# TensorE's order in the state-space scan written out by hand, with dense thirds between its parts

## The chip, the cores and the metric

The kernel runs on one core of one Trainium2 chip. The metric is the device time of one execution in microseconds. The core has a matrix engine (TensorE, PE in the profile, with its weight loads as PEld), a vector engine (VectorE, DVE), a scalar engine (ScalarE, ACT), GpSimd (POOL) and SyncE (SP), which issues most DMAs from one queue. Every engine works its own queue in order; an instruction that waits holds back what stands behind it.

## The reference, cut to what matters

One step of a hybrid decoder layer: a prompt of 1024 tokens and 8 single-token samples. One input projection feeds a state-space branch and a gated-delta branch; gates merge them, and a dense feed-forward and a per-layer input follow. The change lies in the state-space branch:

```python
proj = einsum('bld,de->ble', rms_norm(x), w_in)
z, xbc, dt_raw, qkv, gate, b_raw, a_raw, mgate = split(proj)
xbc = silu(causal_conv(xbc, ...)); xs, bm, cm = split(xbc)
# in chunks of the tokens, h = head, 8 heads in each of 4 groups g
lmat = exp(where(tril, acum_l - acum_s, -inf))            # decay in the chunk
cb = einsum('lgd,sgd->gls', cm, bm)
y_diag = einsum('gls,ghls,sghp->lghp', cb, lmat, xs*dt)   # diagonal product
chunk_states = einsum('lgd,lgh,lghp->ghpd', bm, exp(acum_last - acum), xs*dt)
state = state * exp(acum_last) + chunk_states             # from chunk to chunk
y_off = einsum('lgd,ghpd,lgh->lghp', cm, state_before, exp(acum))
y = (y_diag + y_off + xs * D) * silu(z)
y = rms_norm over each group (y)
```

The reference writes this with chunks of 64; the kernel uses 128.

## The kernel before, in words

**Layout.** Activations lie with channels on the 128 partitions and tokens along the row. Every dense product is done in three passes, with weights and activations each split in a high and a low part. `load_w` brings a weight tile (128 output channels by 1024 inputs, 512 KB) on SyncE's queue into `wraw` (2 buffers); ScalarE casts the high half `wh` (L138) and VectorE subtracts it for `wl` (L139), four of eight blocks at a time, three buffers each. `dense` runs over three thirds of the 1032 tokens (`CHUNKS`, 344 each); a third is 8 blocks times 3 matmuls, 24 in a row into one of three PSUM buffers `pd`, and is then evacuated by `evac`. Other PSUM pools: `pt` (2 buffers: transposes and small products), `py` (2), `pz` (1). All matmuls go through a helper at L69.

**Stages of the state-space branch.** Four groups g of eight heads. For each: `ssm_conv_group` projects and convolves B, C and four tiles X (18 dense thirds; taps on VectorE L411, silu on ScalarE L412, evacuation L397); `ssd` scans eight chunks; `fill` computes the raw output gates that later stages read (four weight tiles in group 0, three in groups 1 to 3, by the table `FILL`), evacuated into `mg` (L270); eight `ssm_dec` decode steps; `ssm_gate` projects four z tiles, multiplies X by silu(z) and sums squares. The root of these is applied beside the next group's convolutions.

**One chunk of `ssd`.** The row of decays is broadcast from DRAM to all partitions (`ab`, 512 KB, DMA L661, pool `sw` with 2 buffers), masked on GpSimd (L662), put through eight exponentials on ScalarE (L666) and multiplied on VectorE by the product CB (L680). The four X tiles are transposed into one `pt` (L669), scaled by VectorE into `xdt` (L672) and `xdd` (L674); CB and the transposed B share another `pt`, B is copied to `btok` (L679). Then the products: the diagonal one into `py` from `ab` and `xdt`; the off-diagonal one into another `py` from the state `st` and C; the chunk's state into `pz` from `btok` and `xdd`. VectorE carries the state on, multiplies the off-diagonal part by `eb` (a second broadcast, L691) and adds the diagonal one into X; GpSimd adds the rest (L711).

**What sets the order.** Nothing is placed by hand in before: the framework's scheduler lays the instructions of the whole program into the engines' queues. The code of `ssd` has no dense work, and `fill` stands behind it; the scheduler puts thirds of the fills between the scan's instructions and ahead of them.

**What precedes.** Ahead of group 0's scan stand the last in-chunk solve of the gated-delta branch (`solve(1)`: 31 steps on VectorE, L542 and L545; its matrix is copied on GpSimd, L547, and put out to DRAM, L548) and the transposes of the gated-delta convolution states (`states`, L419, six of them with four small transposes each, copied on ScalarE at L421 into `cso`, which has one buffer, and put out). Group 3 has the same transposes for the state-space branch. `ssm_dec_start` transposes the decode rows `bdec` and `cdec` (L592).

Of the kernel before, what the change touches and what calls it, by code (L numbers as in the profile page):

```python
# [8 lines left out]
F32 = mybir.dt.float32  # L9
# [7 lines left out]
P = 128  # L17
# [22 lines left out]
def hybrid_step(  # L40
# [108 lines left out]
    def dense(wt, acts, evac, chunks=CHUNKS):  # L149
        n = len(acts)  # L150
        for t0, tn in chunks:
# [8 lines left out]
            evac(t0, tn, o)  # L160

# [106 lines left out]
    def raw_proj(col, dst):  # L268
        t = mgp.tile([P, NT], F32, name="mg")
        dense(load_w(w_in[:, col : col + P], 8), hacts, lambda t0, tn, o: S.copy(t[:, t0 : t0 + tn], o))  # L270
        dma(dst, t)

    def fill(lo, hi):
        """gates of both branches and of the mix, put out as they are"""
        for j in range(lo, hi):
            if j < 16:
                raw_proj(COL_M + j * P, sg_d[j])
            else:
                raw_proj(COL_G + (j - 16) * P, gate_d[j - 16])
# [147 lines left out]
    def gate_proj(col, out, dec, func):  # L427
        def ev(t0, tn, o):
            n = min(tn, NP - t0)
            S.activation(out[:, t0 : t0 + n], o[:, :n], func)  # L430
            if n < tn:
                S.activation(dec, o[:, n:], func)

        dense(load_w(w_in[:, col : col + P], 8), hacts, ev)

# [130 lines left out]
    def norm_small(t, n, group, scale):  # L566
        """reciprocal root of the means of squares over the partitions and `group` tiles."""
# [31 lines left out]
    def ssm_dec(i):  # L599
        """step i: four rows of the batch, one pair of heads"""  # L600
# [34 lines left out]
    with (  # L635
# [19 lines left out]
        def ssd(g, Bt, Ct, X):  # L655
            st = None
            h0 = 8 * g
            for c in range(NC):
                cs = slice(c * C, c * C + C)
                ab = sw.tile([P, 8, C], F32, name="ab")  # L660
                dma(ab, acum_d[h0 : h0 + 8, cs].partition_broadcast(P))  # L661
# [3 lines left out]
                for h in range(8):  # L665
                    S.activation(ab[:, h], ab[:, h], AF.Exp, bias=ncolA[:, c, h0 + h : h0 + h + 1])  # L666
                t = pt.tile([P, 512], F32, name="pt")
# [13 lines left out]
                yd = py.tile([P, 512], F32, name="py")  # L681
                for h in range(8):
# [587 lines left out]
```

## Time and profile before

| | us |
|---|---|
| median of 3 runs | 2751.8 |
| lowest, highest | 2751.22, 2755.93 |
| span of the profiled execution | 2748.0 |
| TensorE busy in it | 2641.6 |
| VectorE, ScalarE, GpSimd busy | 1553.3, 996.6, 247.3 |

The profiled execution's own time is its span, 2748.0 us, and the little that lies around it; the median of the runs is 3.8 us above that span. A row of a timeline gives start, duration, engine, line, operation, the tiles written and read with their shapes, a count, and in brackets the idle time of the engine ahead of it with what ended it. A row of the table by stretches gives the stretch, its width, the busy time (and instructions) of PE, PEld, DVE, ACT and POOL, the clock that TensorE was granted (1.00 is full speed), the mean busy share of the DMA engines, and GB/s. A row of the chain gives start, duration and what the end of the program hung on at that time. Line numbers L are those of the kernel before, unless the changed kernel is named.

### The profile page before, as it was taken

The page shows a single profiled execution, that of the slowest core. Times are in us where ns is not written, and L with a number is a line of the kernel's source. Part 1 is how long each engine was busy: PE and PEld are TensorE (multiplying, and loading weights), DVE is VectorE, ACT ScalarE, POOL GpSimd, SP SyncE. Part 2 cuts the span into 40 slices and gives each one's busy share as a digit, 9 for nine tenths or more (in the row PEclk, how much of TensorE's full clock was granted, in tenths as well). Part 3 has the DMA queues.
Part 4 walks back from the last instruction along what each step waited for, and adds up shares of the span by engine and source line. Part 5 has one row for each costly group of instructions (what it writes and reads, how often), then busy time and mean ns, then how long its engine had stood idle before and what let it go on. Part 6 is the DMA issues. An engine that isn't in the chain of part 4 may idle for free.

```text
span 2748.0 us, 43742 instructions
## 1 busy us (share of the span) xinstructions
PE 2641.6 (96%) x17431; PEld 2551.2 (93%) x17431; DVE 1553.3 (57%) x2754; ACT 996.6 (36%) x2045; POOL 247.3 (9%) x493
## 2 busy tenths in 40 slices
PE   7999999879889889999999999999999999999998
PEld 7999999879779779899999999999999999999998
DVE  6677896767655655663554566434343333333465
ACT  5455544356343343342343225423212121212243
POOL 0101121030210210111010000011000000000020
PEclk9999999999999999999999999999999999999999
DMA  3355443445462462356685438411111111111122
GB/s 122 122 155 175 139 148 111 114 110 154 91 155 85 90 156 85 98 145 195 195 238 166 117 118 272 154 53 47 47 47 43 51 43 51 43 50 43 50 88 92
DMA packets 456665, 306.34 MB, mean 111 GB/s; under 512 B 44049, under 2 KB 430010, under 8 KB 455438
## 3 DMA queue, kind: packets, MB, share of 16 engines
q1 hardware_dynamic: 454062, 295.13, 37.5%
q10 hardware_dynamic: 2400, 8.42, 0.8%
q8 instruction: 137, 2.24, 0.3%
q14 instruction: 66, 0.54, 0.1%
HBM read 227.17 MB, written 76.31 MB: 110 GB/s over the span
## 4 chain that ended last, share of the span: by engine, by line
PE 80%; DMA 8%; DVE 5%; issue 3%; ACT 3%; POOL 1%; SPq 0%; DVEq 0%; POOLq 0%; ACTq 0%
PE pd L69 71%; DMA ab<-acum_d 5%; PE py L69 4%; PE pt L69 2%; PE pz L69 1%; ACT ab L666 1%; POOL ab L662 1%; DVE sd L614 1%; DMA wraw<-in_w_pl_gate_dram 1%; DVE wl L139 1%; DVE sdj L619 1%; DMA sd<-in_state_ssm_dram 0%; ACT wh L138 0%; DMA out_dram<-sd 0%; DMA bc<-bcd_d 0%
## 5 line engine op out<-in xcount | busy, mean ns | idle before, releaser
L69 PE MATMUL pd<-h,wh 128*128 128x344 f32 x6384 | 1552.2, 324 | 7.0 <-ACT wh L138 5.2
L69 PEld LDWEIGHTS pd<-h,wh 128*128 128x128 f32 x6384 | 1112.3, 189 | 24.1 <-issue 11.8
L69 PE MATMUL pd<-h,wl 128*128 128x344 f32 x3192 | 1038.1, 325 | 11.4 <-DVE wl L139 11.0
L69 PEld LDWEIGHTS pd<-h,wl 128*128 128x128 f32 x3192 | 604.3, 189 | 19.7 <-DVE wl L139 14.0
L138 ACT CAST wh<-wraw 128x512 fp32r<-128x512 f32 (+1 forms) x386 | 235.7, 612 | 844.3 <-PE pd L69 821.6
L139 DVE TENSOR_TENSOR wl<-wraw,wh 128x512 fp32r<-128x512 f32 (+1 forms) x386 | 264.8, 687 | 349.4 <-ACT wh L138 339.5
L69 PE MATMUL pd<-gu,wh 128*128 128x344 f32 (+2 forms) x1056 | 249.3, 320 | 0.1
L69 PE MATMUL pd<-y,wh 128*128 128x344 f32 x768 | 186.8, 324 | 0.0
L69 PEld LDWEIGHTS pd<-gu,wh 128*128 128x128 f32 x1056 | 182.4, 188 | 0.5 <-DVE acc L1108 0.4
L69 PE MATMUL pd<-gu,wl 128*128 128x344 f32 (+2 forms) x528 | 168.9, 320 | 0.0
L666 ACT ACTIVATE ab<-ab,ncolA 128x128 f32<-128x128 f32 x256 | 81.0, 392 | 150.7 <-POOL ab L662 150.7
L69 PEld LDWEIGHTS pd<-y,wh 128*128 128x128 f32 x768 | 132.6, 188 | 1.1 <-issue 0.2
L397 ACT COPY raw<-pd 128x344 f32<-128x344 f32 x144 | 63.2, 441 | 180.0 <-PE pd L69 176.2
L69 PE MATMUL pd<-y,wl 128*128 128x344 f32 x384 | 124.9, 325 | 0.0
L1159 DVE TENSOR_TENSOR acc<-acc,pd 128x344 f32<-128x344 f32 x120 | 61.3, 512 | 104.0 <-PE pd L69 103.5
L1138 DVE TENSOR_TENSOR lt<-rb,pd 128x344 f32<-128x344 f32 x66 | 33.9, 513 | 141.4 <-PE pd L69 141.4
L1094 POOL TENSOR_TENSOR sqs<-sqs,sqt 128x1032 f32<-128x1032 f32 x12 | 30.4, 2537 | 923.8 <-ACT sqt L1093 923.8
L69 PEld LDWEIGHTS pd<-gu,wl 128*128 128x128 f32 x528 | 99.2, 188 | 0.0
L411 DVE SCALAR_TENSOR_TENSOR ca<-raw,cwg,ca 128x1056 f32<-128x1056 f32 x72 | 96.3, 1338 | 0.9
L411 DVE SCALAR_TENSOR_TENSOR ca<-raw,cwm,ca 128x1056 f32<-128x1056 f32 x72 | 95.1, 1321 | 1.7
L69 PE MATMUL pd<-h,gw 128*128 128x384 f32 (+1 forms) x576 | 94.3, 322 | 1.7 <-DVE pg L1189 1.7
L69 PEld LDWEIGHTS pd<-h,gw 128*128 128x128 f32 x576 | 91.2, 188 | 2.7 <-DVE pg L1189 2.1
(387 smaller groups left out, 3444.5 us busy)
## 6 DMA issues: line engine op xcount, KB each, us to landing
wraw<-in_w_in_dram SPq DMA_DIRECT2D x88, 512.0 KB
wraw<-in_w_ffn_in_dram SPq DMA_DIRECT2D x44, 512.0 KB
ab<-acum_d SPq DMA_DIRECT2D x32, 512.0 KB
out_dram<-sd SPq DMA_DIRECT2D x48, 256.0 KB
wraw<-in_w_ffn_out_dram SPq DMA_DIRECT2D x40, 256.0 KB
sg_d<-mg SPq DMA_DIRECT2D x16, 516.0 KB
bb<-rk_d SPq DMA_DIRECT2D x8, 1024.0 KB
sd<-in_state_ssm_dram SPq DMA_DIRECT2D x32, 256.0 KB
```

What stands on the lines that cost most here:

```text
L69: TE.matmul(o, l, r, start=start, stop=stop)
L138: S.copy(wh[:, :n], raw[:, k0 : k0 + n])
L139: V.tensor_tensor(wl[:, :n], raw[:, k0 : k0 + n], wh[:, :n].bitcast(F32), ALU.subtract)
L397: S.copy(raw[:, 3 + t0 : 3 + t0 + n], o[:, :n])
L411: V.scalar_tensor_tensor(ca, raw[:, j : j + CONVN], w[j], ca, ALU.mult, ALU.add)
L614: V.scalar_tensor_tensor(s[:, b], s[:, b], dcp[:, pair, bb : bb + 1], u[:, b], ALU.mult, ALU.add)
L619: V.scalar_tensor_tensor(t, s[:, b], 1.0, bcs[1][:, b], ALU.mult, ALU.mult, accum_out=ydec[g][:, i % 4, bb : bb + 1])
L662: G.affine_select(ab, ab, pattern=[[0, 8], [1, C]], compare_op=ALU.is_ge, fill=-1e30, base=0, channel_multiplier=-1)
L666: S.activation(ab[:, h], ab[:, h], AF.Exp, bias=ncolA[:, c, h0 + h : h0 + h + 1])
L1094: G.tensor_tensor(sqs[:, ts], sqs[:, ts], sq[:, :tn], ALU.add)
L1138: V.tensor_tensor(dst[:, t0 : t0 + tn], rb[:, t0 : t0 + tn], o, ALU.mult)
L1159: V.tensor_tensor(a, a, o, ALU.add)
```

## The change

`ssd` becomes a generator in three pieces: `decays(c)` (broadcast, mask and exponentials), `operands(c)` (transposes, CB, `xdt`, `xdd`, `btok`, and the multiply of `ab`) and `products(c)` (state, off-diagonal, diagonal product in this order). The decays of chunks 0 and 1 are issued first, then the operands of chunk 0; after that, for each chunk c, the operands of chunk c+1, the products of chunk c, and the decays of chunk c+2. It yields after each, 17 times in all. `weave` takes from a second generator, at every yield, as many dense thirds as keep step: the fills' thirds and then those of the first two z tiles, 18 thirds in group 0 and 15 in groups 1 to 3. While it runs, TensorE's order is that of the code; the other engines are still laid out by the scheduler. z is copied out raw, and its silu runs later on SBUF in `ssm_gate`; the first two z tiles are projected inside the scan, the other two where they were. The diff also drops comments.

```diff
-    def dense(wt, acts, evac, chunks=CHUNKS):
+    def dense_units(wt, acts, evac, chunks=CHUNKS):
...
             evac(t0, tn, o)
+            yield
+
+    def weave(steps, n_steps, units, n_units):
+        done = 0
+        with tc.manual_schedule(engines={mybir.EngineType.PE}):
+            for i, _ in enumerate(steps):
+                while done < n_units and done * n_steps < (i + 1) * n_units:
+                    next(units, None)
+                    done += 1
+            for _ in units:
+                pass
...
-            S.activation(out[:, t0 : t0 + n], o[:, :n], func)
+            S.copy(out[:, t0 : t0 + n], o[:, :n])
...
+            st = None
+            abs_ = [decays(0), decays(1)]
+            ops = operands(0, abs_[0])
+            yield
+            for c in range(NC):
+                nxt = operands(c + 1, abs_[c + 1]) if c + 1 < NC else None
+                yield
+                st = products(c, st, abs_[c], *ops)
+                if c + 2 < NC:
+                    abs_.append(decays(c + 2))
+                ops = nxt
+                yield
...
+                if i >= len(zs):
+                    for _ in ssm_gate_units(g, i, zs):
+                        pass
+                z = zs[i]
+                S.activation(z, z, AF.Silu)
                 V.tensor_tensor(X[i], X[i], z, ALU.mult)
...
-            ssd(g, Bt, Ct, X)
-            fill(FILL[g], FILL[g + 1])
+            zs = []
+
+            def units():
+                yield from fill_units(FILL[g], FILL[g + 1])
+                for i in range(2):
+                    yield from ssm_gate_units(g, i, zs)
+
+            weave(ssd(g, Bt, Ct, X), 17, units(), 3 * (FILL[g + 1] - FILL[g]) + 6)
```

How the instructions stand now is shown at three places. In a row stand the line, the operation, the tile written (with its number in the program) and the tiles read, the shape, and a count of like instructions. `pd_`, `pt_` are PSUM tiles, `wh_`, `wl_` halves of a weight tile, `h0`, `h1` the activations; lines of the changed kernel are its own (L438, L611, L692, L700 are L419, L592, L669, L677 of before).

TensorE where group 0's scan begins. In before, within a fill's third (`pd_5580`), the transposes of the states (`pt_4414` and on) come one by one between dense matmuls:

```order
L69 MATMUL pd_5580<-h0_101,wh_5546 128x344 x2
L69 MATMUL pd_5580<-h0_101,wl_5547 128x344
L69 MATMUL pd_5580<-h0_101,wh_5546 128x344
L419 MATMUL pt_4414<-ident_78,t_g_804 27x128 x4
L69 MATMUL pd_5580<-h0_101,wh_5546 128x344
L69 MATMUL pd_5580<-h0_101,wl_5547 128x344
```

The same place in after, from behind the last product of the last X tile to the first dense matmul of a fill (`pd_5131`):

```order
L438 MATMUL pt_4414<-ident_78,t_g_804 27x128 x4
L438 MATMUL pt_4423<-ident_78,t_g_804 27x128 x4
L438 MATMUL pt_4432<-ident_78,t_g_804 27x128 x4
L611 MATMUL pt_5071<-ident_78,bdec_393 8x128
L611 MATMUL pt_5071<-ident_78,cdec_394 8x128
L692 MATMUL pt_5105<-ident_78,Xt_4662 128x128
L692 MATMUL pt_5105<-ident_78,Xt_4764 128x128
L692 MATMUL pt_5105<-ident_78,Xt_4866 128x128
L692 MATMUL pt_5105<-ident_78,Xt_4968 128x128
L69 MATMUL pt_5114<-Ct_4560,Bt_4458 128x128
L700 MATMUL pt_5114<-ident_78,Bt_4458 128x128
L69 MATMUL pd_5131<-h0_101,wh_5123 128x344 x2
```

The three state transposes, those of the decode rows and all operands of chunk 0 now stand in one row with no dense matmul between them.

TensorE where group 1's scan begins, in before; `pd_7033` is the last convolution product, `pd_7553` a fill's third:

```order
L69 MATMUL pd_7033<-h1_102,wl_6978 128x344
L592 MATMUL pt_7070<-ident_78,bdec_393 8x128
L592 MATMUL pt_7070<-ident_78,cdec_394 8x128
L669 MATMUL pt_7089<-ident_78,Xt_6661 128x128
L669 MATMUL pt_7089<-ident_78,Xt_6763 128x128
L669 MATMUL pt_7089<-ident_78,Xt_6865 128x128
L69 MATMUL pd_7553<-h0_101,wh_7545 128x344 x2
```

And in after, where `pd_7041` and `pd_7138` are the same:

```order
L69 MATMUL pd_7041<-h1_102,wl_6986 128x344
L611 MATMUL pt_7078<-ident_78,bdec_393 8x128
L611 MATMUL pt_7078<-ident_78,cdec_394 8x128
L692 MATMUL pt_7112<-ident_78,Xt_6669 128x128
L692 MATMUL pt_7112<-ident_78,Xt_6771 128x128
L692 MATMUL pt_7112<-ident_78,Xt_6873 128x128
L692 MATMUL pt_7112<-ident_78,Xt_6975 128x128
L69 MATMUL pt_7121<-Ct_6529,Bt_6427 128x128
L700 MATMUL pt_7121<-ident_78,Bt_6427 128x128
L69 MATMUL pd_7138<-h0_101,wh_7130 128x344 x2
```

The fourth X tile's transpose (`Xt_6975`) now stands ahead of the first fill third, where it stood behind nearly two of them. Group 3 begins with six state transposes in a row (`pt_10911` to `pt_10956`, L438), where before spread four of the six among dense matmuls.

SyncE's queue in group 1's chunks, in before; `ab_` and `eb_` are the two broadcasts of a chunk:

```order
L661 DMA ab_7298<-acum_d_358 128x8x128
L691 DMA eb_7340<-ea_d_359 64x4x128 x2
L661 DMA ab_7357<-acum_d_358 128x8x128
L691 DMA eb_7399<-ea_d_359 64x4x128 x2
L661 DMA ab_7416<-acum_d_358 128x8x128
```

And in after, where `wraw_7843` is a weight tile's load and `mg_7277` a finished gate:

```order
L680 DMA ab_7345<-acum_d_358 128x8x128
L716 DMA eb_7555<-ea_d_359 64x4x128 x2
L146 DMA wraw_7843<-in_w_in_dram 128x8x128
L293 DMA sg_d_371<-mg_7277 128x1032
L680 DMA ab_7457<-acum_d_358 128x8x128
L716 DMA eb_7641<-ea_d_359 64x4x128 x2
```

Loads of weights and the put-out of gates now stand between the chunks' broadcasts.

More of the change, by code (lines that the diff above doesn't have):

```diff
@@ L160, in dense @@
             evac(t0, tn, o)
+            yield
+    def dense(wt, acts, evac, chunks=CHUNKS):
+        for _ in dense_units(wt, acts, evac, chunks):
+            pass
[8 more added lines that the diff above has]
+                pass
     def hilo(h, l, src):
@@ L266, in hybrid_step, with fill_units @@
     mgp = pA.enter_context(tc.tile_pool(name="mgp", bufs=2, reuse_waits="tile"))
[L268 to L271, printed above, removed]
-    def fill(lo, hi):
[L275 to L279, printed above, removed]
+    def fill_units(lo, hi):
+        for j in range(lo, hi):
+            col, dst = (COL_M + j * P, sg_d[j]) if j < 16 else (COL_G + (j - 16) * P, gate_d[j - 16])
+            t = mgp.tile([P, NT], F32, name="mg")
+            wt = load_w(w_in[:, col : col + P], 8)
+            for i, _ in enumerate(dense_units(wt, hacts, lambda t0, tn, o: S.copy(t[:, t0 : t0 + tn], o))):
+                if i == 2:
+                    dma(dst, t)
+                yield
+    def fill(lo, hi):
+        for _ in fill_units(lo, hi):
+            pass
     pC = ExitStack()
@@ L680, in ssd, with products @@
                 V.tensor_tensor(ab, ab, bc(t[:, 0:C], 1, [P, 8, C]), ALU.mult)
-                yd = py.tile([P, 512], F32, name="py")
-                for h in range(8):
-                    hh, i = h % 2, h // 2
-                    mm(yd[64 * hh : 64 * hh + 64, i * C : i * C + C], xdt[:, h], ab[:, h])
+                return xdt, xdd, bt
+            def products(c, st, ab, xdt, xdd, bt):
+                cs = slice(c * C, c * C + C)
+                ps = pz.tile([P, 512], F32, name="pz")
+                mm(ps, bt, xdd.rearrange("p h q -> p (h q)"))
                 if c > 0:
@@ L703, in ssd @@
                     V.tensor_tensor(sn, sn, ps, ALU.add)
-                st = sn
+                yd = py.tile([P, 512], F32, name="py")
+                for h in range(8):
+                    hh, i = h % 2, h // 2
+                    mm(yd[64 * hh : 64 * hh + 64, i * C : i * C + C], xdt[:, h], ab[:, h])
                 for i in range(4):
```

32 lines of the change are left out of this document (19 added, 13 removed).

## The prediction, on record before the changed kernel ran

> **What bounds the kernel now.** I read the totals and the chain first, then TensorE's waits, then the clock and the busy time of the four stretches that the change touches. The page's totals, and its chain by engine and by line:
>
> ```profile
> PE 2641.6 (96%) x17431; PEld 2551.2 (93%) x17431; DVE 1553.3 (57%) x2754; ACT 996.6 (36%) x2045; POOL 247.3 (9%) x493
> PE 80%; DMA 8%; DVE 5%; issue 3%; ACT 3%; POOL 1%; SPq 0%; DVEq 0%; POOLq 0%; ACTq 0%
> ```
>
> TensorE is busy 96% of the span, so only its idle time and its slowed time can be won. What it waits for between 475 and 1235 us (total, times, longest):
>
> ```profile
> PE py L69 <- DVE ab L680: 29.9, 15, 5.7
> PE pz L69 <- DVE btok L679: 20.7, 9, 5.7
> PE pd L69 <- DVE wl L139: 11.0, 5, 4.3
> ```
>
> Nearly all its waits are the scan's: the decay matrix `ab`, the token-major `btok` behind it on VectorE, and the weight splits. Each row below runs from the end of a group's convolution products to the next stage (width, busy time by engine, clock, DMA share):
>
> ```profile
> 475.30:632.50 157.20, 134.74 (x860) 123.90 (x860) 111.88 (x223) 75.91 (x164) 30.87 (x43) 0.92 0.47 122
> 702.10:838.70 136.60, 119.23 (x769) 108.64 (x767) 80.89 (x207) 54.17 (x146) 23.22 (x40) 0.93 0.57 124
> 907.80:1045.20 137.40, 117.24 (x769) 107.20 (x767) 80.19 (x207) 54.35 (x146) 23.69 (x40) 0.94 0.52 123
> 1114.10:1234.30 120.20, 114.05 (x794) 104.46 (x792) 80.56 (x207) 53.18 (x136) 22.18 (x37) 1.00 0.49 131
> ```
>
> I count as lost the width less PE's busy time, plus (1 − clock) × width. Group 0: 22.5 + 12.6 = 35.1 us. Group 1: 17.4 + 9.6 = 27.0. Group 2: 20.2 + 8.2 = 28.4. Group 3: 6.2 + 0. These 96.7 us are all that a better order could win; TensorE's work is the same before and after. The rows for its pieces, from the chain and from PE's timeline:
>
> ```profile
> 1894.50 712.72 PE pd L69 x4516
> 724.95 2.07 PE L69 MATMUL pz<-xdd,btok 128*128 128x512 f32 x2 [2.77 <-DVE btok L679]
> 739.54 1.02 PE L69 MATMUL pz<-xdd,btok 128*128 128x512 f32 x2
> 752.96 1.09 PE L69 MATMUL py<-ab,xdt 128*64 128x128 f32 x16 [0.42 <-DVE ab L680]
> 753.99 1.16 PE L69 MATMUL py<-Ct,st 128*128 128x128 f32 x8
> 754.98 0.39 PE L69 MATMUL pt<-Ct,Bt 128*128 128x128 f32 x2
> 755.31 0.60 PE L669 MATMUL pt<-ident,Xt 128*128 128x128 f32 x4
> 755.67 0.41 PE L69 MATMUL pd<-h,wl 128*128 128x344 f32 x1
> 720.00:740.00 20.00, 17.23 (x117) 14.25 (x116) 14.57 (x27) 6.28 (x19) 6.29 (x11) 0.91 0.63 137
> ```
>
> 712.72/4516 = 0.158 us a dense matmul, so a third of a weight tile (24 of them) is 3.79 us. From start to start a chunk's own work is 1.03 + 0.99 + 0.33 + 0.36, with the state product's 1.02: 3.7 us. A wait also slows what follows it: after 2.77 us idle the state product took 2.07 instead of 1.02, and the 20 us slice with that one wait has clock 0.91, so a cold start costs about 20 × 0.09 = 1.8 us beyond the idle time.
>
> [...]
>
> **The order written out.** In before, the fills' dense thirds lie among the transposes and ahead of the chunks. In after, nothing dense stands between a group's last convolution product and its first operands, and one third then follows each half step. A chunk takes 2 × 3.79 + 3.7 = 11.3 us where TensorE sets the pace. So there is a term for each group's beginning, and one for waits inside the chunks.
>
> *Group 0's beginning.* The first diagonal product needs `ab`, whose broadcast stands on SyncE's queue behind the put-out of the last solve's matrix:
>
> ```profile
> 487.43 0.69 DVE L139 TENSOR_TENSOR wl<-wraw,wh 128x512 fp32r<-128x512 f32 x1
> 521.45 0.68 DVE L139 TENSOR_TENSOR wl<-wraw,wh 128x512 fp32r<-128x512 f32 x1
> 523.95 1.16 DVE L545 TENSOR_REDUCE xs<-stmp 128x31 f32<-128x961 f32 x1
> 525.02 0.68 DVE L672 TENSOR_TENSOR xdt<-pt,colB 128x512 f32<-128x512 f32 x1
> 525.16 2.03 POOL L547 COPY blk<-xs 128x1024 f32<-128x1024 f32 x1 [43.37 <-DVE xs L545]
> 527.22 0.32 SPq L548 DMA_DIRECT2D dd_d<-blk  x1
> 527.63 9.68 DMA ab<-acum_d
> 537.43 1.09 POOL L662 TENSOR_SCALAR_AFFINE_SELECT ab<-ab 128x1024 f32<-128x1024 f32 x1 [10.24 <-DMA ab<-acum_d]
> 538.56 2.46 ACT L666 ACTIVATE ab<-ab,ncolA 128x128 f32<-128x128 f32 x8 [2.21 <-POOL ab L662]
> 541.12 1.22 DVE L680 TENSOR_TENSOR ab<-ab,pt 128x1024 f32<-128x1024 f32 x1 [4.64 <-ACT ab L666]
> L138 ACT CAST wh<-wraw 128x512 fp32r<-128x512 f32 (+1 forms) x386 | 235.7, 612 | 844.3 <-PE pd L69 821.6
> ```
>
> Six weight splits (the first and last are shown) run inside the solve, six times about 0.62 from start to start = 3.7 us; the fills that they serve come later in after, so the solve ends near 521.4, the copy of `blk` near 523.5. Then 10.2 to POOL's select, 1.1, 2.5 for eight exponentials with two casts of 0.61 that the order puts among them, 1.2 for the multiply: 539.9 us. From 475.3 that is 64.6 us, in which TensorE now has only three thirds (11.4), the transposes and two chunks' operands and a state product (together 3.7): 49.5 us lost, and 1.8 for the cold start behind it: 51.3. Inside it are two waits of their own. Three state transposes stand in a row, two `pt` buffers hold them, and each is freed by a copy of ScalarE into one buffer that DMA empties:
>
> ```profile
> 492.39 0.57 ACT L421 COPY cso<-pt 27x512 f32<-27x512 f32 x1
> 494.89 0.58 ACT L421 COPY cso<-pt 27x512 f32<-27x512 f32 x1 [1.09 <-DMA out_dram<-cso]
> 1115.14 0.57 ACT L421 COPY cso<-pt 27x512 f32<-27x512 f32 x1
> 1117.72 0.58 ACT L421 COPY cso<-pt 27x512 f32<-27x512 f32 x1 [2.00 <-DMA out_dram<-cso]
> 1120.41 1.06 ACT L412 ACTIVATE Xt<-ca 128x1024 f32<-128x1024 f32 x1 [0.33 <-DVE ca L411]
> ```
>
> Copies come at least 2.5 us apart, so the first third starts near 491; and chunk 1's transposes want the buffer that `xdt` of chunk 0 frees behind the solve, near 522. Both end before 539.9 and add nothing to it. Before had twelve thirds (45.5 us) over this stretch. That cover is what is gone; it serves the chunks afterwards.
>
> *Groups 1 and 2.* The fourth X tile is convolved behind the last product:
>
> ```profile
> 702.74 0.43 ACT L397 COPY raw<-pd 128x336 f32<-128x336 f32 x1
> 707.17 0.45 ACT L270 COPY mg<-pd 128x344 f32<-128x344 f32 x1 [3.69 <-PE pd L69]
> 709.48 1.06 ACT L412 ACTIVATE Xt<-ca 128x1024 f32<-128x1024 f32 x1 [1.86 <-DVE ca L411]
> ```
>
> Before laid a third and more over it. In after TensorE waits from 702.1 to near 709.1 (the fill's copy at 707.17, which held the silu back, comes later), less 0.7 of operands: 6.3 + 1.8 = 8.1 us.
>
> *Group 3* has the same and six state transposes in a row: copies near 1115.1, 1117.7, 1121.5 (behind the silu of 1120.41), 1124.1, 1126.7, 1129.3; the first third at 1130.2. From 1114.1 that is 16.1, less 2.9 of work, 13.2 + 1.8 = 15.0 us.
>
> *Inside the chunks.* `ab` has two buffers: the broadcast for chunk c goes out when chunk c−2 is done. The sixteen waits on it in the chain run between these two:
>
> ```profile
> 735.85 11.93 DMA ab<-acum_d
> 1174.59 6.60 DMA ab<-acum_d
> ```
>
> Sixteen have a mean near 9.0. With 1.1 + 2.5 + 1.2 and 0.7 of handing over, the multiply ends about 14.5 us after chunk c−2; it frees the `pt` buffer that the operands of c+1 take, which TensorE reaches 15.5 us after c−2 where a third stands ahead, and 11.6 where none does. Groups 1 to 3 spread 15 thirds over 17 steps, so one place (the operands of chunk 5) has none: 2.9 us there, 5.4 if SyncE is held for one set of exponentials (2.46) by a weight load ahead of that broadcast, whose buffer comes free by casts behind them; I take 4, between the two, and 1.8 cold. VectorE queues the weight splits behind these multiplies: an estimate of 2 a group, between nothing and the 11.0 of the waits above. The tail, two z tiles and decode steps without fills, 2, from nothing to two such thirds. So 9.8 in groups 1 to 3 and 5.8 in group 0, which has 18 thirds, enough for every step; it has the cold start once.
>
> **z put out raw.** Sixteen silus on SBUF at 1.06 us (the row at 709.48) are added on ScalarE; evacuation becomes a copy of the same size. Table loads between exponentials and silus fall away:
>
> ```profile
> L666 ACT ACT_TABLE_LOAD x12 | 15.4, 1283 | 0.1
> ```
>
> ScalarE is busy 54 us of 137 in a group, so I cost both at nothing: z's silu is covered by the decode steps and the next group's convolution products. Queue order on SyncE, the sums of squares and everything else stay at nothing likewise; VectorE is at 80 of 137.
>
> **The sum.** Group 0: 51.3 + 5.8 = 57.1 against 35.1, +22.0. Groups 1 and 2: 17.9 against 27.0 and 28.4, −9.1 and −10.5. Group 3: 24.8 against 6.2, +18.6. Together +21.0. The profiled execution has 2748.0 of span, and the median of the runs, 2751.8, lies 3.8 above, which I add: 2769.0 + 3.8 = 2773 us, 0.8% slower. With nothing inside the chunks the sum is −14.2: 2738.
>
> **Rivals.** *The broadcast sets the pace (slower still).* Two chunks then take the latency plus 5.5 to the end of the multiply plus 7 from there (a third and 3.2 of the chunk's own): 12.5 + latency. At 9.0 this is 21.5, under 22.6; from 10.1 it decides; at 11.93 each chunk takes 12.2, 0.9 more, over some 28 chunks 25 us: 2798. The DMA share of 0.47 to 0.57 and the 11.93 speak for it; that chunks are spread out more speaks against.
>
> *The thirds cover every wait (faster).* With broadcasts at 6.60 even the place without a third lacks only 0.5 us, splits are not held, and the time is 2738. It needs the inner waits to stay under 14.2 us in all, of the 35 I put there; under that, faster. Group 3 of before, with broadcasts of 6.60, loses but 6.2, which speaks for it.
>
> *Gain and loss cancel (no change).* With inner waits near 14, some 3.5 a group, 2752 ± 5.5; 0.2% or 5.5 us is about what a measurement of this kernel can tell from no change.
>
> *The clock stays up after short waits.* If waits as short as those of chunk 5 do not slow the clock, the three 1.8 there fall away: 2773 − 5.4 = 2768. The row at 724.95, slowed after 2.77 us, is against it. [...]
>
> **How the numbers follow.** My forecast, slower by 8 to 33 us, 0.42; the clock's variant 0.05; the pace set by broadcasts 0.18; cancelling 0.15; covered 0.20. The range reaches from the covered case to the slow one, 2738 to 2800; the likeliest's own is 2760 to 2785. Faster 0.20, same 0.15, slower 0.65.
>
> **What would show it.** Right: TensorE idle most of 475 to 540, a wait of `pt` on `xdt` ending near 522 and of `py` on `ab` near 540; pauses of 6 us in groups 1 and 2 and 13 in group 3; few waits of `py` on `ab` later. Wrong: group 0's first diagonal product well before 540, if its broadcast needs less than 9 or stands elsewhere on the queue; or clock 1.00 in groups 1 and 2; or periods above 12 us in the chunks.

## The result, and the profile after

The changed kernel took 2794.2 us (median of 4 runs, 2791.5 to 2797.7) where before took 2751.6: a ratio of 1.0145, 95% interval 1.0128 to 1.0162. The forecast was 2773 with a range of 2738 to 2800: the direction was right, half of the loss was foreseen, and the result lies near the upper end of the range. The profiled execution has a span of 2789.8 us, 41.8 above that of before. Its totals:

```profile
PE 2645.4 (95%) x17431; PEld 2560.2 (92%) x17431; DVE 1557.5 (56%) x2756; ACT 1010.6 (36%) x2067; POOL 249.4 (9%) x493
```

The work is the same (17431 matmuls, 2645 us busy, some of it at a lower clock, 0.65 to 0.97 in the stretches below); the rest is waiting. What TensorE waits for now, in total, times, longest (L692, L700 are the transposes, L695 `xdt`, L703 the multiply of `ab`, L438 and L440 the states' transposes and their copy, L754 the transposes of a group's final state):

```profile
PE pt L692 <- DVE xdt L695: 22.2, 1, 22.2
PE pt L69 <- DVE ab L703: 20.5, 4, 6.9
PE pt L438 <- ACT cso L440: 14.7, 6, 3.8
PE pt L692 <- ACT Xt L431: 13.4, 2, 6.7
PE py L69 <- DVE ab L703: 8.3, 1, 8.3
PE pt L754 <- DVE st L726: 5.6, 2, 4.3
```

Of before's three kinds of waits (29.9, 20.7 and 11.0 us) the first two are gone in their old form: no product waits on `btok`, and only one diagonal product waits on `ab` (8.3 us). New ones stand at the beginnings of groups and at the products CB. The same by stretches, each group's beginning and its remainder apart (width, busy by engine, clock, DMA share, GB/s):

```profile
475.20:540.50 65.30, 23.00 (x103) 18.95 (x103) 50.67 (x78) 12.24 (x30) 4.88 (x7) 0.66 0.32 86
540.50:670.20 129.70, 120.32 (x782) 112.00 (x783) 68.03 (x170) 60.99 (x150) 24.38 (x36) 0.95 0.52 119
734.30:742.60 8.30, 1.62 (x10) 1.39 (x9) 6.32 (x8) 2.28 (x6) 0.76 (x4) 0.74 0.52 127
742.60:876.00 133.40, 120.90 (x795) 113.94 (x795) 73.29 (x189) 63.36 (x152) 23.97 (x36) 0.94 0.48 113
947.70:1076.00 128.30, 118.49 (x799) 110.94 (x798) 73.44 (x189) 63.16 (x151) 24.33 (x36) 0.96 0.52 118
1139.00:1157.00 18.00, 8.12 (x39) 5.33 (x38) 8.31 (x11) 5.65 (x12) 0.51 (x2) 0.65 0.17 46
1157.00:1310.00 153.00, 146.93 (x993) 139.83 (x993) 85.63 (x216) 61.78 (x150) 27.49 (x51) 0.97 0.51 136
```

In group 0 TensorE stands idle for 42 of the first 65 us, the hole that before had filled with twelve thirds.

For the comparison of all kernels I use the time from a group's last evacuation of a convolution product to the first one of the next group (for group 3: to the end of the program), read from ScalarE's timeline of each profiled execution:

| kernel | ratio to before (95%) | group 0 | group 1 | group 2 | group 3 to end |
|---|---|---|---|---|---|
| before | 1 | 167.0 | 139.8 | 140.6 | 1633 |
| changed (after) | 1.0145 (1.0128–1.0162) | 195.0 | 141.7 | 136.6 | 1650 |
| e1_g0free: group 0 not woven | 1.0135 (1.0118–1.0152) | 186.8 | 141.4 | 136.3 | 1650 |
| e2_even: thirds spread evenly | 1.0161 (1.0145–1.0176) | 196.5 | 142.5 | 143.3 | 1654 |
| e4_rawz: before, z raw | 1.0008 (0.9998–1.0017) | 165.4 | 140.0 | 140.4 | 1640 |
| e5_g0old: group 0 by the old scan | 1.0042 (1.0026–1.0059) | 167.5 | 143.5 | 139.6 | 1652 |
| e6_head: two thirds ahead | 1.0109 (1.0086–1.0131) | 198.9 | 135.7 | 135.5 | 1649 |
| e7_states: state transposes moved | 1.0163 (1.0148–1.0178) | 199.7 | 143.6 | 139.5 | 1646 |
| e8_ab3: three buffers of `ab` | 1.0067 (1.0046–1.0088) | 191.0 | 135.9 | 137.3 | 1647 |
| e9_before_ab3: before, three buffers | 0.9970 (0.9962–0.9979) | 167.2 | 140.6 | 136.8 | 1631 |
| e10_mix: the mix | 0.9869 (0.9852–0.9886) | 163.2 | 127.3 | 124.7 | 1635 |
| e11_abpool: broadcast from GpSimd | 1.0281 (1.0268–1.0294) | 212.8 | 149.5 | 148.1 | 1657 |
| e12_g0lead: mix, group 0 woven | 0.9889 (0.9864–0.9913) | 175.4 | 128.9 | 125.5 | 1634 |
| e13_g3woven: mix, group 3 woven | 0.9853 (0.9831–0.9875) | 166.3 | 127.8 | 123.9 | 1635 |

Each stage is from one execution, which is not always near the median of its kernel (that of e1 was its fastest of four, those of e2 and e8 their slowest). The woven but otherwise unedited group 1 of after, e1 and e5 reads 141.4 to 143.5, group 2 136.3 to 139.6, and the unedited group 0 of after, e2 and e6 195.0 to 198.9, so I read nothing from a difference under 4 us. The last column holds 1600 us of later work and scatters by some 7 (e4_rawz, whose group 3 is nearly that of before). Kernels ran on different chips, on which before took 2752 to 2762; so totals are compared by their ratios, and a us given for one below is its ratio times 2751.6.

### The profile page after: what moved, and what is told of

Same layout as the page of the kernel before. It is cut to its first block, busy times and chain, and to the rows that moved or that the text cites. A ratio compares the mean times of both kernels' runs of the same rounds, so it can differ in the third digit from the quotient of the medians.

```text
span 2789.8 us, 43759 instructions
## 1 busy us (share of the span) xinstructions
PE 2645.4 (95%) x17431; PEld 2560.2 (92%) x17431; DVE 1557.5 (56%) x2756; ACT 1010.6 (36%) x2067; POOL 249.4 (9%) x493
## 4 chain that ended last, share of the span: by engine, by line
PE 65%; DMA 6%; DVE 4%; ACT 3%; issue 1%; POOL 0%; SPq 0%; DVEq 0%; POOLq 0%; ACTq 0%
PE pd L69 57%; PE py L69 3%; DMA ab<-acum_d 3%; PE pt L69 2%; PE pz L69 1%; ACT ab L685 1%; DMA out_dram<-so 1%; DVE sdj L638 1%; DVE sd L633 1%; DMA bc<-bcd_d 0%; DVE ca L430 0%; DVE wl L139 0%; DMA wraw<-in_w_pl_gate_dram 0%; ACT wh L138 0%; DMA mg<-y_d 0%
## 5 line engine op out<-in xcount | busy, mean ns | idle before, releaser
L685 ACT ACTIVATE ab<-ab,ncolA 128x128 f32<-128x128 f32 x256 | 81.8, 390 | 174.7 <-POOL ab L681 174.6
```

## The experiments

### The weaving taken out of group 0

```diff
-            weave(ssd(g, Bt, Ct, X), 17, units(), 3 * (FILL[g + 1] - FILL[g]) + 6)
+            if g == 0:
+                for _ in ssd(g, Bt, Ct, X):
+                    pass
+                for _ in units():
+                    pass
+            else:
+                weave(ssd(g, Bt, Ct, X), 17, units(), 3 * (FILL[g + 1] - FILL[g]) + 6)
```

> The changed kernel, but group 0's scan and its thirds are not woven: TensorE's order in group 0 is left to the scheduler, groups 1 to 3 stay woven. My theory: the hand order takes away the thirds that covered the solve's end and the first broadcast. From the last convolution evacuation of group 0 to the first of group 1 it was 167.0 us before and 195.0 after; it should come back to 167 to 172, and the time from 2794 to 2763 to 2772. Rival: the thirds only move, and what group 0 gains at its beginning it loses again inside its chunks: 2785 or more.

My theory failed, and the rival's time came out. Group 0 came from 195.0 to 186.8, not to 167; the total to 1.0135, not told apart from after. The hole before 540 us is gone (TensorE is busy 54 of the 60 us from 480 to 540), but the chunks now wait. TensorE's waits in this kernel's group 0:

```profile
PE pz L69 <- DVE st L726: 12.5, 2, 7.3
PE pt L69 <- DVE ab L703: 10.6, 3, 4.6
PE pd L69 <- ACT zt L449: 7.6, 1, 7.6
```

Two of them on its timeline, and on VectorE's queue the late instruction ahead of each add that they wait for, with the second add:

```profile
587.64 2.07 PE L69 MATMUL pz<-xdd,btok 128*128 128x512 f32 x2 [5.11 <-DVE st L726]
617.00 2.08 PE L69 MATMUL pz<-xdd,btok 128*128 128x512 f32 x2 [7.35 <-DVE st L726]
...
585.44 0.69 DVE L717 TENSOR_TENSOR eb<-eb,py 128x512 f32<-128x512 f32 x1 [6.11 <-DMA eb<-ea_d]
614.26 1.22 DVE L703 TENSOR_TENSOR ab<-ab,pt 128x1024 f32<-128x1024 f32 x1 [2.39 <-ACT ab L685]
...
616.26 0.68 DVE L726 TENSOR_TENSOR st<-st,pz 128x512 f32<-128x512 f32 x1
```

The state's product of the next chunk has one `pz` buffer, which the state's add (L726) frees. On VectorE's queue that add stands in the first wait behind the multiply of `eb`, in the second behind the next chunk's multiply of `ab`, and both multiplies are late with a broadcast. The code of before also has `eb` ahead of the add; the next chunk's `ab` ahead of it comes with the operands issued one chunk ahead. My reading was that this code brings a chain of its own, whoever orders TensorE. That became the next theory.

### Group 0 by the scan code of before

Edit: for `g == 0` the function `ssd` of before is called (operands and products of a chunk together), then the units; groups 1 to 3 stay woven.

```diff
-            weave(ssd(g, Bt, Ct, X), 17, units(), 3 * (FILL[g + 1] - FILL[g]) + 6)
+            if g == 0:
+                ssd_old(g, Bt, Ct, X)
+                for _ in units():
+                    pass
+            else:
+                weave(ssd(g, Bt, Ct, X), 17, units(), 3 * (FILL[g + 1] - FILL[g]) + 6)
```

> The changed kernel, but group 0 is scanned by the code of before (operands and products of a chunk together, diagonal product first, left to the scheduler), its fills and first two z tiles behind it; groups 1 to 3 stay woven. The run without the weaving in group 0 alone gave back 8 of 28 us in group 0. Theory one: the other 20 us come from the code with operands one chunk ahead, whose products wait for the state's add behind the next chunk's multiply of ab on VectorE; then group 0's stage falls from 187 to 165 to 170 and the time to 2760 to 2769. Rival: they come from z's thirds standing ahead of the decode steps, which leaves the scheduler less to cover with; then the stage stays above 180, the time above 2778.

Theory one held: group 0 takes 167.5 us, as in before, and the ratio falls to 1.0042 (28 us less than after). The thirds are the same as in the run above and in the same place in the code, so z's thirds are not the cause. Taken out in this order, group 0's 28 us divide into about 8 for TensorE's order by hand and 19 for the scan's code; the code of before under an order by hand was not tried, so the division may fall otherwise. Which of that code's parts (operands ahead, or the diagonal product put last) weighs more was not tried alone either.

### Thirds spread evenly in groups 1 to 3

```diff
-            weave(ssd(g, Bt, Ct, X), 17, units(), 3 * (FILL[g + 1] - FILL[g]) + 6)
+            weave(ssd(g, Bt, Ct, X), 17 if g == 0 else 15, units(), 3 * (FILL[g + 1] - FILL[g]) + 6)
```

> The changed kernel with the 15 thirds of groups 1 to 3 given to the first 15 of the 17 steps, one each, so that the operands of chunk 5 have a third ahead of them and the two last steps have none. My theory: the three waits of CB on the multiply of ab (6.0, 6.9 and 4.5 us) go, with cold starts of about 2 us each: 17 to 24 us, so 2770 to 2778. Rival: two buffers of ab and the broadcast's latency set the pace, and the wait comes back one chunk later: 2788 or more.

A miss: 1.0161, no gain. The waits that it was aimed at did fall; others took their place. TensorE's waits in groups 1 to 3 of this kernel:

```profile
PE pd L69 <- ACT wh L138: 8.9, 7, 1.9
...
PE pt L69 <- DVE ab L703: 5.7, 3, 3.4
PE pz L69 <- DVE st L726: 5.1, 2, 2.7
PE pd L69 <- ACT zt L449: 4.4, 2, 2.4
PE pd L69 <- DVE wl L139: 4.0, 6, 0.8
```

The CB waits are 5.7 instead of the 17.4 of chunk 5 (6.0 + 6.9 + 4.5), but dense thirds now wait for weight casts (8.9 where after has 0.8 in these groups), evacuations and splits, which stand behind exponentials and multiplies that wait for a broadcast. One of them: TensorE waited 1.28 us, to 819.27, for the cast at 818.62, which stood on ScalarE behind exponentials that had waited 7.50 us for GpSimd's mask. So the rival's time came out, though not by a wait one chunk later alone: what comes next on these queues inherits the late decays.

### Three buffers for the decays

```diff
-                ab = sw.tile([P, 8, C], F32, name="ab")
+                ab = sw.tile([P, 8, C], F32, name="ab", bufs=3)
...
-            sqs = s1.tile([P, NP], F32, name="sqs")
+            sqs = s1.tile([P, NP], F32, name="sqs", tag="sq")
...
-            rb = s1.tile([P, NP], F32, name="srb")
+            rb = s1.tile([P, NP], F32, name="srb", tag="sq")
```

> The changed kernel with three buffers of ab instead of two (the broadcast for a chunk may start a chunk earlier; room for it comes from one buffer shared by the sums of squares and the roots' broadcast). My theory: the waits of CB and of the final transposes on the multiply of ab (20.5 and 5.6 us with their cold starts) fall by more than half, 12 to 30 us: 2764 to 2782. Rival: the decays are held by the queues of SyncE, ScalarE and VectorE and not by the buffer: 2788 or more.

Held: 1.0067, 21 us less than after. In groups 1 and 2 no CB waits on `ab` any more; what is left in group 1 is mainly the beginning, the final transposes and casts:

```profile
PE pt L692 <- ACT Xt L431: 6.7, 1, 6.7
PE pt L754 <- DVE st L726: 4.5, 1, 4.5
PE pd L69 <- ACT wh L138: 2.8, 2, 1.5
```

The final transposes wait as in after, against the expectation: there are no thirds left at the end, and more buffers do not change that. With the third buffer no CB wait on `ab` is left in groups 1 to 3 either, so it was having only two buffers of `ab` that made these waits. Their going did not shorten every stage: group 2 stayed at 137.3 us, where waits for weight casts (4.1), splits (2.8) and final transposes (3.0) take the place of the 6.9 of CB.

### The broadcast issued from GpSimd

```diff
-                dma(ab, acum_d[h0 : h0 + 8, c * C : c * C + C].partition_broadcast(P))
+                for q in range(0, 8, 4):
+                    G.dma_start(ab[:, q : q + 4], acum_d[h0 + q : h0 + q + 4, c * C : c * C + C].partition_broadcast(P))
```

> The changed kernel with the broadcasts of ab issued from GpSimd's queue, in two halves, so that no weight load on SyncE's queue stands ahead of them; two buffers as in the changed kernel. Theory: of the 6.0, 6.9 and 4.5 us of waits in chunk 5 about 2.6 each come from that hold: 8 to 12 us with cold starts, 2782 to 2787. Rival: the hold is not SyncE's but the buffer's and the broadcast's own time: 2790 to 2798; slower still if issuing on GpSimd delays its adds and masks.

Much slower, 1.0281. GpSimd's timeline in group 1 shows why the run does not answer its question:

```profile
784.12 0.77 POOL L681 DMA_DIRECT2D ab<-acum_d  x1
790.12 0.46 POOL L738 TENSOR_TENSOR Xt<-Xt,eb 128x128 f32<-128x128 f32 x1 [5.23 <-DVE Xt L733]
790.52 0.78 POOL L681 DMA_DIRECT2D ab<-acum_d  x1
```

The second half of a broadcast stands behind an add into X that waits 5.23 us for VectorE, so it starts 6.4 us after the first. One queue's hold was exchanged for a longer one. That SyncE held the broadcast in after is read from its own timeline (below), not shown by this run.

### Two thirds ahead of the operands in groups 1 to 3

```diff
+            for _ in range(2 if g else 0):
+                yield
             ops = operands(0, abs_[0])
...
-            weave(ssd(g, Bt, Ct, X), 17, units(), 3 * (FILL[g + 1] - FILL[g]) + 6)
+            weave(ssd(g, Bt, Ct, X), 19 if g else 17, units(), 3 * (FILL[g + 1] - FILL[g]) + 6)
```

> The changed kernel with two of the 15 thirds of groups 1 to 3 put ahead of chunk 0's operands, the other 13 spread over the 17 steps. Theory one (thirds are a fixed supply): TensorE's waits of 6.7 us on the fourth X tile go in groups 1 and 2, and about the same comes back inside the chunks, where four places instead of two have no third: 2788 to 2800. Rival: the beginning is a loss of its own: 2 times 8 us and 2 to 8 in group 3 go, 2770 to 2779.

Between the two: 1.0109, some 10 us less than after, though the two intervals just overlap. Group 1 fell by 6.0 us, group 2 by 1, which is nothing. The waits on the fourth X tile are gone, and those of CB rose. TensorE's waits in group 2 of this kernel:

```profile
PE pt L69 <- DVE ab L703: 9.5, 3, 4.9
PE pt L756 <- DVE st L726: 2.9, 1, 2.9
```

Three CB waits of 9.5 us in all stand where after had one of 6.9. Thirds are a limited supply, but in group 1 not a fixed sum: there two thirds at the beginning are worth more than two in the chunks.

### The states' transposes moved

```diff
-        solve(1)
         gdnc.states(conv)
+        solve(1)
...
-            if g == 3:
-                ssmc.states(conv)
...
             weave(ssd(g, Bt, Ct, X), 17, units(), 3 * (FILL[g + 1] - FILL[g]) + 6)
+            if g == 3:
+                ssmc.states(conv)
```

> The changed kernel with the transposes of the convolution states elsewhere: in group 0 they are issued ahead of the last solve, in group 3 behind the woven scan. My theory: in group 0 they cost nothing, since the solve's end and the broadcast set the first diagonal product (540.5 us): its stage stays at 195 within 2 us; in group 3 8 to 13 us fall away: 2781 to 2787. Rival: they cost in group 0 too what TensorE waited for them there, 10 us more: 2771 to 2777.

With group 0's transposes behind its woven scan as well (e3_states, on the same expectation) the order of the instructions deadlocks, so there is no time for that form. In this one, the gain that the rival expected in group 0 did not come; its stage took 199.7 us, 2.7 more than the expectation allowed, and unedited ones reach 198.9. TensorE's timeline of this kernel, where group 0's last convolution copy starts at 484.1 instead of 475.6:

```profile
490.90 0.48 PE L692 MATMUL pt<-ident,Xt 128*128 128x128 f32 x1 [6.89 <-ACT Xt L431]
532.53 1.11 PE L692 MATMUL pt<-ident,Xt 128*128 128x128 f32 x4 [31.90 <-DVE xdt L695]
550.82 1.97 PE L69 MATMUL py<-ab,xdt 128*64 128x128 f32 x16 [8.90 <-DVE ab L703]
```

What TensorE no longer waits for a copy of the states it waits for `xdt`, behind the solve: 31.9 instead of 22.2 us. The first diagonal product comes 66.7 us after the last convolution copy, in after 64.9. But the whole stage moved: convolutions end 8.5 us later and the solve 10.8 us later than in after, so the run shows where the wait goes, not that the transposes are free. In group 3 the time to the end fell by 5 us where 8 to 13 were expected, within the scatter of that column; the wait on the fourth X tile (6.9) that the transposes had covered came out. The total, 1.0163, is no better than after and misses the expectation.

### z raw alone

On the kernel before:

```diff
-            S.activation(out[:, t0 : t0 + n], o[:, :n], func)
+            S.copy(out[:, t0 : t0 + n], o[:, :n])
...
                 gate_proj(COL_Z + (4 * g + i) * P, z, zdec[:, 4 * g + i], AF.Silu)
+                S.activation(z, z, AF.Silu)
```

> The kernel before with one part of the change alone: z is evacuated by a copy and its silu runs on SBUF afterwards (on each z tile, and once per group on the decode rows). My theory: nothing that can be measured, 2746 to 2757, since ScalarE is busy 54 of 137 us in a group. Rival: 16 silus of 1.06 us lie on the path of the last z tile's multiply: up to 17 us, 2769. Other rival: table loads between exponentials and silus fall away on ScalarE's path to the decays, 14 us: 2738.

Ratio 1.0008 (0.9998 to 1.0017): nothing that can be told from no change, as costed. The table loads ahead of exponentials and z's silu did fall in this kernel, from 12 + 11 to 8 + 7, without an effect on the time.

### Three buffers in before, and mixes

```diff
-                ab = sw.tile([P, 8, C], F32, name="ab")
+                ab = sw.tile([P, 8, C], F32, name="ab", bufs=3)
...
-            sqs = s1.tile([P, NP], F32, name="sqs")
+            sqs = s1.tile([P, NP], F32, name="sqs", tag="sq")
...
-            rb = s1.tile([P, NP], F32, name="srb")
+            rb = s1.tile([P, NP], F32, name="srb", tag="sq")
```

> The kernel before with three buffers of ab and nothing else (the buffer shared by squares and roots makes the room). Theory: the waits on ab and btok (29.9 and 20.7 us with cold starts, in all groups) come from broadcasts that cannot start until the chunk two before is done; with a third buffer they fall by a third or more: faster by 15 to 35 us. Rival: the scheduler's thirds already cover what can be covered and the decays are held by the queues: within 6 us of before.

Faster by 0.3% (0.9970), 8 us: less than the theory's 15 to 35, a little more than the rival's 6. `ab` waits fell to 10.5 us in all, `btok` waits rose to 29.2:

```profile
PE pz L69 <- DVE btok L679: 29.2, 10, 7.0
PE pd L69 <- DVE wl L139: 12.6, 6, 4.3
PE py L69 <- DVE ab L680: 10.5, 6, 2.7
```

The mix of what the runs had favoured: `ssd_old` (the scan code of before) in groups 0 and 3, weaving in 1 and 2 with two thirds ahead, three buffers. The buffer edit and the two steps ahead are those shown above; the rest is:

```diff
-            weave(ssd(g, Bt, Ct, X), 17, units(), 3 * (FILL[g + 1] - FILL[g]) + 6)
+            if g in (0, 3):
+                ssd_old(g, Bt, Ct, X)
+                for _ in units():
+                    pass
+            else:
+                weave(ssd(g, Bt, Ct, X), 19, units(), 3 * (FILL[g + 1] - FILL[g]) + 6)
```

> A mix meant to beat both: groups 0 and 3 scanned by the code of before and left to the scheduler, groups 1 and 2 woven with two thirds ahead of their first operands, three buffers of ab everywhere, z raw as in the changed kernel. Theory: group 0's and 3's stages as in before or better (167, and 1633 from group 3's begin to the end), groups 1 and 2 near 132 each against 140: 2725 to 2742 where before has 2752. Rival: what weaving wins in groups 1 and 2 is given back by z's thirds missing around the decode steps: 2750 or more.

Faster than both, 0.9869 (0.9852 to 0.9886), 36 us under before by that ratio and so 10 better than the theory's best. Groups 1 and 2 of this kernel by stretch:

```profile
703.50:830.80 127.30, 119.62 (x809) 111.49 (x808) 79.10 (x196) 64.64 (x156) 23.45 (x40) 0.97 0.58 130
893.50:1018.20 124.70, 118.03 (x804) 109.86 (x803) 79.89 (x196) 64.74 (x156) 23.80 (x40) 0.99 0.61 131
```

And TensorE's waits in its group 1 (L756 are the final transposes here):

```profile
PE pt L756 <- DVE st L726: 6.1, 1, 6.1
PE pd L69 <- ACT wh L138: 0.8, 1, 0.8
PE pd L69 <- DVE wl L139: 0.4, 1, 0.4
```

With the beginning covered and the buffer there, only the final transposes still wait, and the clock is 0.97 and 0.99 instead of 0.93 and 0.94 of before. Three buffers alone gave 5.8 us in group 1 of the woven kernel, two thirds ahead 6.0, both 14.4; in group 2 neither changed much (136.6 against 137.3 and 135.5), both 11.9. TensorE's waits in group 2 say how: 16.5 us in after, 14.3 with two thirds ahead, 16.6 with three buffers, 6.3 with both. Each part alone moved the wait to another place. Without the weaving three buffers gave nothing that can be told from the scatter (+0.8 and −3.8 us, e9_before_ab3).

Group 0 of the mix woven too, twelve thirds ahead, `weave0` giving one at each of them and six over the other steps (edit against the mix):

```diff
-            for _ in range(2 if g else 0):
+            for _ in range(2 if g else 12):
                 yield
...
-            if g in (0, 3):
+            if g == 3:
                 ssd_old(g, Bt, Ct, X)
...
+            elif g == 0:
+                weave0(ssd(g, Bt, Ct, X), units())
```

> The mix (groups 1 and 2 woven with two thirds ahead, group 3 by the code of before, three buffers of ab) with group 0 woven too: its twelve fill thirds stand ahead of chunk 0's operands, the six of z are spread over the scan. The mix had 2717.9 us where before had 2754.1, and 163.2 us in group 0's stage. Theory: thirds are a fixed supply, and the twelve that cover the solve are missing in the chunks; the six state transposes still stand ahead of them: 175 to 190 in the stage, 2730 to 2746. Rival: only the missing cover at the beginning was wrong with weaving group 0; with it the stage is 160 to 168 and the time 2715 to 2724.

Its stage takes 175.4 us, at the edge of the theory's 175 to 190, and 12 more than with the code of before (163.2). The total does not confirm it: 0.9889 is not told apart from the mix's 0.9869, and at the 2754.1 of the expectation's before it is 2724 us, under the theory's 2730. TensorE has no wait of its own on the states' copies there, against what I expected. The longest waits in the stage are those of a diagonal product on `ab` (7.9 us) and of the state's product on the state's add (7.6 us, 6.6 of it behind a multiply of `ab`), the chain of e1_g0free again. Weaving group 0 with cover costs less than weaving it bare (191.0 with three buffers), but in its stage still loses.

Group 3 of the mix woven as groups 1 and 2 are (edit against the mix):

```diff
-            if g in (0, 3):
+            if g == 0:
                 ssd_old(g, Bt, Ct, X)
...
-            if g == 3:
-                ssmc.states(conv)
...
+            if g == 3:
+                ssmc.states(conv)
```

> The mix with group 3 woven as groups 1 and 2 are (two thirds ahead, three buffers of ab), the states' transposes behind its scan. Theory: before lost only 6.2 us there, so weaving has nothing to win: from group 3's last convolution to the end 1635.4 becomes 1635 to 1645, the time 2718 to 2728. Rival: group 3 gains as groups 1 and 2 did, 10 us or more: 2708 or less.

It changes nothing that can be told: 1634.9 from group 3 to the end against 1635.4, the ratio 0.9853 (0.9831 to 0.9875) beside 0.9869. As in the theory, there was nothing to win. Weaving as such did not cost group 3 its 17 us in after, then; cover at the beginning, the moved transposes and the third buffer together bring them back, and which of them counts is not shown.

## Why the prediction was right, and where it fell short

**Group 0's beginning held to the microsecond.** The working put chunk 1's transposes near 522, the end of the copy of `blk` at 523.5 and the first diagonal product at 539.9; the copy ended at 523.1. TensorE's timeline of after:

```profile
521.79 1.11 PE L692 MATMUL pt<-ident,Xt 128*128 128x128 f32 x4 [22.17 <-DVE xdt L695]
540.50 1.97 PE L69 MATMUL py<-ab,xdt 128*64 128x128 f32 x16 [8.27 <-DVE ab L703]
```

The shift of the solve by the six splits and the broadcast behind the put-out of `blk` were right. The last step was close by some compensation: the mask came 11.4 us after the copy of `blk` where 10.2 stood in the sum. That the states' transposes add nothing to it is read from the first line: TensorE still waited 22.17 us behind them.

**Groups 1 and 2's beginnings** were put at 6.3 us of wait: 6.7 each. **Group 3** was put 18.6 us worse than before; it is 17 worse, and its first third came 16.4 us after the last convolution product where 16.1 was put.

**Inside the chunks is the step that failed in size.** The terms "9.8 in groups 1 to 3 and 5.8 in group 0", with one cold start of 1.8 a group behind the beginning, make 42.4 us together. From the stretches above, width less busy and (1 − clock) × width: 9.4 + 6.5 in group 0, 12.5 + 8.0 in group 1, 9.8 + 5.1 in group 2, 6.1 + 4.6 in group 3, 62.0 us. That is 20 of the 21 us missing between +21.0 and +41.8. By groups, from one group's last convolution copy to the next group's last, the time changed by +32, 0, −7 and +17 us, where +22.0, −9.1, −10.5 and +18.6 stood in the sum. (The working itself says that group 0 has the cold start once, but adds 1.8 in both of its terms.) In group 0 the larger waits inside the chunks were for weight casts (4.5 us), for CB (3.1) and for an evacuation (1.3).

In group 1, 12.5 us of idle time stand where 8 were put, and 8.0 of slowed clock where 3.6 were. The named place, chunk 5, was found, with the hold on SyncE's queue that the prediction gave as the upper end. In after the diagonal product of the chunk two before ended at 776.7; a weight load stood ahead of the broadcast until the casts behind the exponentials were done, and a gate's put-out behind that load (rows of TensorE, ScalarE, SyncE, VectorE and TensorE again):

```profile
775.58 1.09 PE L69 MATMUL py<-ab,xdt 128*64 128x128 f32 x16
...
777.68 0.60 ACT L138 CAST wh<-wraw 128x512 fp32r<-128x512 f32 x1
...
778.22 0.38 SPq L146 DMA_DIRECT2D wraw<-in_w_in_dram  x1
778.70 0.53 SPq L293 DMA_DIRECT2D sg_d<-mg  x1
779.32 0.38 SPq L680 DMA_DIRECT2D ab<-acum_d  x1
...
793.19 1.22 DVE L703 TENSOR_TENSOR ab<-ab,pt 128x1024 f32<-128x1024 f32 x1 [8.86 <-ACT ab L685]
794.56 0.77 PE L69 MATMUL pt<-Ct,Bt 128*128 128x128 f32 x2 [5.97 <-DVE ab L703]
841.59 1.12 PE L754 MATMUL pt<-ident,st 128*128 128x128 f32 x4 [4.29 <-DVE st L726]
```

The hold was 2.6 us (776.7 to 779.32) and the mask came 10.2 after the broadcast's issue, where a broadcast of 9.0 was taken; so the wait was 5.97 where I took 4. Between two ends I chose the middle, and the upper end, 5.4, was the case and a little more. The final transposes waited 4.29, which "the tail, 2" had too small; and the three waits of the group (6.7, 5.97, 4.29) each brought a cold start (pairs of dense matmuls at 0.78 us instead of 0.48, until 744.9, 799.6 and 847.6), where the sum had two. I costed the waits as if they stood alone; the queues of ScalarE and VectorE hand them on, as the row of e2_even above shows.

**Where the range was lucky.** The forecast's own range was 2760 to 2785; 2794 lies above it. The upper end of 2800 came from the rival in which the broadcast sets the pace, and that mechanism did not occur. That the range holds the result is owed in part to a case that was not the one.

**The rivals.** The broadcast did not set the period: chunks with a third at each half step came 11.3 us apart (diagonal products at 764.26, 775.58 and 786.91 in group 1). The covered case did not come. A third buffer (e8_ab3) meets its premise in part: no CB wait in groups 1 to 3, but waits for casts (6.9 us), splits (3.8) and final transposes (7.5) remain there, 18.2 us together and so more than the 14.2 that this case allows, and the time stayed above before's. The clock's variant fails: after the wait of 3.12 us in after's group 0, dense pairs took 0.78 us instead of 0.48 for some 3 us, and the 10 us from 600, with no wait in them, had a granted clock of 0.91:

```profile
597.62 0.46 PE L69 MATMUL pt<-Ct,Bt 128*128 128x128 f32 x2 [3.12 <-DVE ab L703]
...
599.40 0.78 PE L69 MATMUL pd<-h,wh 128*128 128x344 f32 x2
...
602.40 0.48 PE L69 MATMUL pd<-h,wh 128*128 128x344 f32 x2
```

**z put out raw.** It was costed at nothing, and e4_rawz agrees. But the reason given, that table loads between exponentials and silus fall away, does not hold in the changed kernel: 14 loads ahead of exponentials and 13 ahead of z's silu (L685, L771) stand where before had 12 and 11.

**Not foreseen at all** was that the scan's new code costs group 0 some 19 us where the scheduler orders TensorE (e1_g0free against e5_g0old): the prediction priced positions of thirds and left VectorE's queue at 2 us a group. A state's add behind the next chunk's decays is seen there in one wait of 7.35 us; how the rest of the 19 us arises is not shown.

## What to carry to other kernels

An order written out by hand replaces cover that a scheduler had found; before pricing what the new order hides, list what lay over each beginning (a solve, a convolution, a row of copies) and where that cover goes. Issuing an operand one step ahead also moves its consumers' neighbours on other engines' queues (here a state's add behind the next chunk's decays, a wait of 7.35 us in e1_g0free): ask what stands behind the operand that is late, and give the late transfer a buffer first. Here the same weaving, a loss of 1.5% as it came, was part of a gain of 1.3% once it was confined to groups 1 and 2, which have no solve or row of state transposes at their beginning, had two thirds ahead of the first operands, and a third buffer for the decays. Of that gain, 0.3% came with the buffer alone.

## What the runs showed of the hardware

Two waits, of 3.12 and 5.97 us, cost TensorE some 2 us more behind them. From CB over one third to the state's product it took 4.15 us without a wait (547.35 to 551.50 in after), 5.72 behind the wait of 3.12 us (597.62 to 603.34) and 6.58 behind the wait of 5.97 us (794.56 to 801.14): 1.6 and 2.4 us more, around the 1.8 that the prediction took for a cold start. After 5.97 us idle, pairs of dense matmuls took 0.78 us instead of 0.48 from 796 to 799.6, and the 10 us from 794 had a granted clock of 0.71. In e11_abpool a DMA issued by GpSimd took 0.77 us of that engine, and the second half of a broadcast, behind an add that waited 5.23 us, came 6.4 us after the first.
